# A two-layer hybrid transformer block on one core: where the recurrence's query decays and running totals are computed

## The chip, the cores and the metric

One core of a Trainium2 chip runs the whole program in one launch. The metric is the device time of one execution in microseconds (us), median of the runs shown. The engines are named as the profile names them: PE (TensorE, matrix products), PEld (its weight loads), DVE (VectorE), ACT (ScalarE), POOL (GpSimd) and SP (SyncE, which issues nearly all transfers).

## The reference

Two layers over 1024 latent tokens and 256 context tokens of width 1024. Each layer normalises, projects every token into eleven groups of columns (neighbourhood attention q, k, v; the recurrence's q, two forget gates, values and output gate; three inputs of a short convolution), mixes them in three ways, projects back, and runs a 16-expert layer. The change lies in the recurrence (HGRN2): six heads of 64 channels, forward and backward, a gated scan in chunks.

```python
def step(s, xs):
    qc, kc, gc, vc = xs
    a = jnp.cumsum(gc, axis=2)
    diff = a[:, :, :, None, :] - a[:, :, None, :, :]
    decay = jnp.exp(jnp.where(causal[:, :, None], diff, -jnp.inf))
    scores = jnp.sum(qc[:, :, :, None, :] * kc[:, :, None, :, :] * decay, axis=-1)
    o = jnp.einsum('bhts,bhsv->bhtv', scores, vc) + jnp.einsum('bhtk,bhkv->bhtv', qc * jnp.exp(a), s)
    ...
    s_new = jnp.exp(a_last[:, :, 0, :, None]) * s + jnp.einsum('bhsk,bhsv->bhkv', kc * jnp.exp(a_last - a), vc)
    return s_new, o
```

## The kernel before

A layer runs in stages: normalisation (`norm1`), the mixers' projections with the recurrence and the convolution (`mixers_in`), the projections for attention (`na_proj`), attention (`na_prep`, `na_pair`), the output projection, the experts. The program is recorded in this order, and then a scheduler that plays it through with its own table of costs decides in which order each engine's instructions stand; at run time each engine takes them strictly in that order. So the matmuls of the projections (`proj_ch`, L277, and `proj_tok`, L288, both writing `pj`) stand between the small products of the recurrence on PE.

The recurrence of a layer: three pairs of heads (`hg_pair`, p = 0, 1, 2), in each pair two heads one after the other, in each head two groups of 640 tokens (`hg_group`, g = 0, 1), whose instructions the scheduler interleaves. That makes 12 groups a layer and 24 in all. Channels of the forward direction lie in partitions 0 to 63 (`lo`), those of the backward direction in 64 to 127 (`hi`). A group goes through seven levels, h = 1, 2, 4, ..., 64, and at each level pairs of neighbouring blocks of h tokens are joined:

- up to h = 16, the half of the keys that is wanted is copied into `kz` (ACT L354, DVE L355), PE multiplies `kz` with the queries `Qt` (`small`, 20 products of 32x32, L341) and DVE merges the result into `Pc` (L357). At h = 32 and 64 PE multiplies `Kt` and `Qt` directly (L365) and ACT and DVE copy out (`Pf`, L370, L372).
- then half of the keys is multiplied by the neighbouring block's total decay (DVE, two instructions of 64x320, L375 and L376), half of the queries likewise (POOL, two of 64x320, L377 and L378), and the totals of neighbouring blocks are multiplied into the totals of the next level (`tot`, POOL L380, of 128x320 at the first level and half as wide at each further one).

The products of the next level read the new `Qt`, and the new `Qt` may only be written once the products of this level have read the old. After the levels the keys are transposed (L388), multiplied with the values (L393), and the states `S` are chained on DVE (`hg_states`, L411). When both heads of a pair are done, PE forms the outputs `ho` (L493, L496) and their mean squares `hms` (L505), DVE takes the reciprocal (L508), POOL multiplies (L509) and SP stores `mix`.

`wgroup` splits each weight into a high and a low part for the projections: `whi` on ACT (L264), `wlo` on DVE (L265). After the last pair of heads the convolution (`conv`, DVE L546 and L549, POOL L539 and L556) uses the recurrence's buffers. When these are released, attention's tables (`cw`, `sw`, L609 and L610) and its inputs (`qk`, L661) are loaded, normalised (`nsq`, `nss`, `nrsy`, `qd`) and transposed on PE (`nt`, L697). In attention's first part PE also forms the modulation vectors (`aps`, L157) from weights `wm` that SP loads (L153).

Of the kernel before, what the change touches and what calls it, by code (L numbers as in the profile page):

```python
# [15 lines left out]
ALU = mybir.AluOpType  # L16
# [26 lines left out]
class Kern:  # L43
# [283 lines left out]
    def hg_group(self, l, hd, g, F, Kt, Qt, S):  # L327


        nc, hp = self.nc, self.hp  # L330
# [3 lines left out]
        lo, hi = slice(0, 64), slice(64, 128)  # L334
# [14 lines left out]
        while h < P:  # L349
            n2 = G // (2 * h)  # L350
            v = lambda t: t.rearrange("p (n two h) -> p n two h", two=2, h=h)
# [21 lines left out]
            tv = tot.rearrange("p (n two) -> p n two", two=2)  # L373
            bc = lambda s, i: tv[s, :, i:i + 1].to_broadcast([64, n2, h])
            nc.vector.tensor_tensor(v(Kt)[lo, :, 0], v(Kt)[lo, :, 0], bc(lo, 1), ALU.mult)  # L375
            nc.vector.tensor_tensor(v(Kt)[hi, :, 1], v(Kt)[hi, :, 1], bc(hi, 0), ALU.mult)  # L376
            nc.gpsimd.tensor_tensor(v(Qt)[lo, :, 1], v(Qt)[lo, :, 1], bc(lo, 0), ALU.mult)  # L377
            nc.gpsimd.tensor_tensor(v(Qt)[hi, :, 0], v(Qt)[hi, :, 0], bc(hi, 1), ALU.mult)  # L378
            nt = hp.tile([P, n2], F32, name=f"tot{h}", bufs=1 if h < 64 else 4)
            nc.gpsimd.tensor_tensor(nt, tv[:, :, 0], tv[:, :, 1], ALU.mult)  # L380
            tot = nt
            h *= 2

# [1155 lines left out]
```

## Time and profile before

| | |
|---|---|
| median of 3 runs | 2754.39 us (2744.39 to 2755.64) |
| the profiled execution | 2748.93 us, span 2747.2 us |
| granted TensorE clock, mean | 0.959 of full speed |
| PE busy | 2520.3 us, 92% of the span |
| DVE busy | 1800.3 us, 66% |
| ACT busy | 1132.7 us, 41% |
| POOL busy | 1050.2 us, 38% |
| recurrence, layer 0 | about 165 to 572 us |
| recurrence, layer 1 | about 1613 to 2004 us |

PE's busy time counts an instruction from its start to a modelled end. A wait is put down to the instruction whose signal came last. The windows of the two layers run from the first product of the first head to the last `hms`.

### The profile page before, as it was taken

Reading aid. Unit: us, or ns where it says so; the run is one execution under the profiler, and the core shown is the slowest. Engines: PE = TensorE matmul, PEld = TensorE weight load, DVE = VectorE, ACT = ScalarE, POOL = GpSimd, SP = SyncE. Lnnn points to the kernel's source line nnn. Section 1 sums busy time; section 2 is a strip of 40 time slices with the busy share of each in tenths; the row PEclk is TensorE's granted clock in tenths of the full one; section 3 lists DMA queues with packets and bytes.
Section 4 is the critical chain, followed back from the end, with each engine's and each line's share of the span. In section 5 each row is a group of like instructions: output and inputs, shape, how many; then the busy total and the mean of one; then the engine's idle time right before and its main releaser. Section 6 shows DMA issues by size and latency. Waiting matters only on the chain.

```text
span 2747.2 us, 55415 instructions
## 1 busy us (share of the span) xinstructions
PE 2520.3 (92%) x21959; PEld 1923.8 (70%) x21959; DVE 1800.3 (66%) x3542; ACT 1132.7 (41%) x1878; POOL 1050.2 (38%) x1125
## 2 busy tenths in 40 slices
PE   7999999988999979999997999999879899589997
PEld 4988877885577855555554988778864677357664
DVE  4247776756777487777754347677767774687874
ACT  4224434324554534444433324344324454445452
POOL 1035454534544733323321035355554442222242
PEclk9999999998999979999998999999989899789999
DMA  7332324246444857888887332323176355779994
GB/s 277 104 105 71 103 72 124 64 140 209 150 141 148 302 190 261 285 271 296 262 279 231 90 109 72 114 76 103 50 208 222 100 164 185 283 269 369 378 376 129
DMA packets 347938, 507.14 MB, mean 185 GB/s; under 512 B 53380, under 2 KB 203072, under 8 KB 346592
## 3 DMA queue, kind: packets, MB, share of 16 engines
q1 hardware_dynamic: 336416, 465.85, 50.1%
q0 software_dynamic: 11264, 37.75, 5.9%
q8 instruction: 173, 2.83, 0.4%
q14 instruction: 85, 0.70, 0.1%
HBM read 410.10 MB, written 94.90 MB: 184 GB/s over the span
## 4 chain that ended last, share of the span: by engine, by line
PE 71%; DVE 15%; DMA 5%; issue 3%; ACT 2%; POOL 2%; SPq 1%; POOLq 0%; DVEq 0%; ACTq 0%
PE pj L277 15%; PE pg L1280 13%; PE pd L1335 8%; PE pj L288 8%; PE po L828 6%; PE nao L786 3%; PE npt L762 2%; PE pgc L1265 2%; DVE Kt L375 2%; PE aps L157 2%; PE hl L341 1%; PE sA L733 1%; DVE Kt L376 1%; DVE kz L355 1%; PE hl L365 1%
## 5 line engine op out<-in xcount | busy, mean ns | idle before, releaser
L1182 DVE TENSOR_TENSOR ewl<-est,ewh 128x2048 fp32r<-128x2048 f32 x126 | 298.3, 2371 | 112.6 <-ACT ewh L1178 108.1
L1178 ACT CAST ewh<-est 128x2048 fp32r<-128x2048 f32 x128 | 243.5, 1906 | 173.6 <-PE pg L1280 122.6
L277 PE MATMUL pj<-hl,whi 128*128 128x320 f32 (+2 forms) x912 | 314.2, 345 | 0.0
L277 PE MATMUL pj<-hh,whi 128*128 128x320 f32 (+2 forms) x912 | 312.5, 343 | 0.7 <-ACT pev L420 0.7
L277 PE MATMUL pj<-hh,wlo 128*128 128x320 f32 (+2 forms) x912 | 312.9, 343 | 0.0
L288 PE MATMUL pj<-whi,hh 128*128 128x256 f32 x960 | 279.8, 292 | 8.8 <-ACT nev L566 8.5
L288 PE MATMUL pj<-whi,hl 128*128 128x256 f32 x960 | 276.4, 291 | 0.9 <-DVE hl L239 0.9
L288 PE MATMUL pj<-wlo,hh 128*128 128x256 f32 x960 | 276.3, 289 | 0.0
L1335 PE MATMUL pd<-est,hidT 128*128 128x512 f32 x512 | 232.2, 596 | 2.1 <-ACT hidT L1302 2.1
L288 PEld LDWEIGHTS pj<-whi,hh 128*128 128x128 f32 x960 | 187.7, 195 | 12.0 <-ACT nev L566 9.3
L288 PEld LDWEIGHTS pj<-wlo,hh 128*128 128x128 f32 x960 | 187.5, 195 | 2.2 <-issue 1.5
L288 PEld LDWEIGHTS pj<-whi,hl 128*128 128x128 f32 x960 | 185.7, 195 | 3.8 <-DVE hl L239 1.5
L377 POOL TENSOR_TENSOR Qt<-Qt,tot 64x320 f32<-64x320 f32 x144 | 128.8, 894 | 150.9 <-PE hl L341 93.5
L277 PEld LDWEIGHTS pj<-hh,whi 128*128 128x128 f32 x912 | 174.8, 192 | 14.4 <-ACT pev L420 1.0
L277 PEld LDWEIGHTS pj<-hl,whi 128*128 128x128 f32 x912 | 174.9, 192 | 14.0 <-issue 1.2
L277 PEld LDWEIGHTS pj<-hh,wlo 128*128 128x128 f32 x912 | 175.0, 192 | 13.7 <-issue 1.4
L752 POOL TENSOR_SCALAR S<-S,sm 128x768 f32<-128x768 f32 (+2 forms) x108 | 112.7, 1045 | 186.3 <-DVE sm L751 153.2
L1335 PEld LDWEIGHTS pd<-est,hidT 128*128 128x128 f32 x512 | 95.2, 189 | 110.7 <-issue 103.3
L265 DVE TENSOR_TENSOR wlo<-wst,whi 128x1024 fp32r<-128x1024 f32 (+1 forms) x72 | 81.6, 1149 | 138.5 <-ACT whi L264 137.7
L1280 PE MATMUL pg<-ewh,xh 128*128 128x512 f32 x512 | 157.0, 425 | 2.9 <-ACT xh L1235 2.8
L1280 PE MATMUL pg<-ewl,xh 128*128 128x512 f32 x512 | 147.6, 404 | 0.0
L375 DVE TENSOR_TENSOR Kt<-Kt,tot 64x320 f32<-64x320 f32 x144 | 96.5, 670 | 76.7 <-POOL tot L380 39.6
(369 smaller groups left out, 5857.5 us busy)
## 6 DMA issues: line engine op xcount, KB each, us to landing
est<-in_w_exp_gate_dram SPq DMA_DIRECT2D x64, 1024.0 KB
est<-in_w_exp_up_dram SPq DMA_DIRECT2D x64, 1024.0 KB
est<-in_w_exp_down_dram SPq DMA_DIRECT2D x64, 1024.0 KB
wm<-in_w_mod_dram SPq DMA_DIRECT2D x80, 512.0 KB
wst<-in_w_in_dram SPq DMA_DIRECT2D x88, 256.0 KB
pna<-nev SPq DMA_DIRECT2D x180, 64.0 KB
wos<-in_w_out_dram SPq DMA_DIRECT2D x42, 256.0 KB
mst<-mix SPq DMA_DIRECT2D x32, 320.0 KB
```

What stands on the lines that cost most here:

```text
L265: nc.vector.tensor_tensor(b, c, a, ALU.subtract)
L277: nc.tensor.matmul(ps[:, :cn], sel(a(k)), b[:, k, c0:c0 + cn], start=n == 0, stop=n == 3 * KD - 1)
L288: nc.tensor.matmul(ps[:, :2 * P], b[:, k, t * P:(t + 1) * P], a(k).rearrange("p a n -> p (a n)"), start=n == 0, stop=n == 3 * KD - 1)
L375: nc.vector.tensor_tensor(v(Kt)[lo, :, 0], v(Kt)[lo, :, 0], bc(lo, 1), ALU.mult)
L377: nc.gpsimd.tensor_tensor(v(Qt)[lo, :, 1], v(Qt)[lo, :, 1], bc(lo, 0), ALU.mult)
L752: nc.gpsimd.tensor_scalar(S[:, :w], S[:, :w], sm[:, 1:2], 1.0, ALU.mult, ALU.mult)
L786: nc.tensor.matmul(po[64 * X:64 * X + 64, gi], V[:kn, tt, 64 * X:64 * X + 64], PT[X][:kn, i], start=i == 0, stop=i == len(ch) - 1, tile_po ...
L828: nc.tensor.matmul(ps, a, b, start=n == 0, stop=n == len(ops) - 1)
L1178: nc.scalar.copy(hi, src)
L1182: nc.vector.tensor_tensor(lo[:, :m], src[:, :m], hi[:, :m], ALU.subtract)
L1280: nc.tensor.matmul(acc[gu], a[:, 4 * hf + k], b[:, 512 * k:512 * k + 512], start=n == 0, stop=n == 3 * KD - 1)
L1335: self.downed = nc.tensor.matmul(po[nn], hT[:, 2 * hf + k], st[:, c:c + 512], start=hf == 0 and k == 0, stop=hf == 1 and k == 1)
```

## The change

The two multiplications of `Qt` by the decays and the multiplication of the totals, at every level of every group, are issued to VectorE instead of GpSimd. Operands, sizes and count stay: 14 multiplications of 64x320 and 7 of `tot` a group.

```diff
@@ -374,10 +374,10 @@
             bc = lambda s, i: tv[s, :, i:i + 1].to_broadcast([64, n2, h])
             nc.vector.tensor_tensor(v(Kt)[lo, :, 0], v(Kt)[lo, :, 0], bc(lo, 1), ALU.mult)
             nc.vector.tensor_tensor(v(Kt)[hi, :, 1], v(Kt)[hi, :, 1], bc(hi, 0), ALU.mult)
-            nc.gpsimd.tensor_tensor(v(Qt)[lo, :, 1], v(Qt)[lo, :, 1], bc(lo, 0), ALU.mult)
-            nc.gpsimd.tensor_tensor(v(Qt)[hi, :, 0], v(Qt)[hi, :, 0], bc(hi, 1), ALU.mult)
+            nc.vector.tensor_tensor(v(Qt)[lo, :, 1], v(Qt)[lo, :, 1], bc(lo, 0), ALU.mult)
+            nc.vector.tensor_tensor(v(Qt)[hi, :, 0], v(Qt)[hi, :, 0], bc(hi, 1), ALU.mult)
             nt = hp.tile([P, n2], F32, name=f"tot{h}", bufs=1 if h < 64 else 4)
-            nc.gpsimd.tensor_tensor(nt, tv[:, :, 0], tv[:, :, 1], ALU.mult)
+            nc.vector.tensor_tensor(nt, tv[:, :, 0], tv[:, :, 1], ALU.mult)
             tot = nt
             h *= 2
```

The scheduler gives another order for it, and not on DVE and POOL alone.

DVE in layer 1, first head of the third pair, one group at h = 4 and the other at h = 1 (`Pc` is the merge of a level's products, `hmm` its mask). Before:

```order
L357 COPY_PREDICATED Pc<-hmm_16124,hl 128x160
L375 TENSOR_TENSOR Kt<-Kt,tot_20464 64x160x2
L376 TENSOR_TENSOR Kt<-Kt,tot_20464 64x160x2
L357 COPY_PREDICATED Pc<-hmm_16116,hl 128x160
L355 COPY kz_16152<-Kt 64x80x4
L375 TENSOR_TENSOR Kt<-Kt,tot_20494 64x80x4
L376 TENSOR_TENSOR Kt<-Kt,tot_20494 64x80x4
```

The same place now:

```order
L357 COPY_PREDICATED Pc<-hmm_16124,hl 128x160
L377 TENSOR_TENSOR Qt<-Qt,tot_20235 64x80x4
L378 TENSOR_TENSOR Qt<-Qt,tot_20235 64x80x4
L355 COPY kz_16152<-Kt 64x80x4
L357 COPY_PREDICATED Pc<-hmm_16116,hl 128x160
L377 TENSOR_TENSOR Qt<-Qt,tot_20464 64x160x2
L378 TENSOR_TENSOR Qt<-Qt,tot_20464 64x160x2
L376 TENSOR_TENSOR Kt<-Kt,tot_20295 64x20x16
L380 TENSOR_TENSOR tot_20494<-tot_20464 128x160
L375 TENSOR_TENSOR Kt<-Kt,tot_20494 64x80x4
L376 TENSOR_TENSOR Kt<-Kt,tot_20494 64x80x4
```

Each merge is now followed by the two query decays of its group, and a total stands right ahead of the key decays that read it.

PE in layer 1, where the projections end and attention's transposes begin. Before, 240 matmuls of L288 stand between the last `hms` (L505) and the first transposes (`nt`). There the rows are

```order
L288 MATMUL pj<-whi,hl 128x256
L697 MATMUL nt<-idf,qd 128x128 x20
L735 MATMUL sB<-KH,QT 128x256
L735 MATMUL sB<-KL,QT 128x256
L157 MATMUL aps<-wm,sT 32x512 x6
L697 MATMUL nt<-idf,qd 128x128 x8
```

Now 46 matmuls of L288 are left after the last `hms`, and the rows are

```order
L288 MATMUL pj<-whi,hl 128x256
L157 MATMUL aps<-wm,sT 32x512 x8
L697 MATMUL nt<-idf,qd 128x128 x4
L157 MATMUL aps<-wm,sT 32x512 x8
L697 MATMUL nt<-idf,qd 128x128 x8
L157 MATMUL aps<-wm,sT 32x512 x2
```

So 194 matmuls of the projections have moved ahead of the recurrence's end, and 16 of the modulation ahead of most of the first transposes. At the same place of layer 0 it is 444 before and 310 now, and the modulation stays behind.

SP in layer 1, behind the last store of the recurrence's output. Before:

```order
L510 DMA mix_15766<-hos 128x512
L568 DMA pna_15767<-nev 128x128 x2
L596 DMA naw<-in_na_q_norm_dram 128x64
L597 DMA naw<-in_na_k_norm_dram 128x64
L609 DMA cw<-in_rope_dram 128x4x64
```

Now:

```order
L510 DMA mix_15766<-hos 128x512
L869 DMA wr<-in_w_router_dram 128x8x16
L637 DMA E<-rpbx 64x14x64 x4
L596 DMA naw<-in_na_q_norm_dram 128x64
L597 DMA naw<-in_na_k_norm_dram 128x64
L609 DMA cw<-in_rope_dram 128x4x64
```

The stores of the projections (`pna`) are done by then, and the loads of `wr` and `E` have come ahead of the tables.

## Rows read from the trace of the kernel before

**Rows 1.** The page: busy time by engine, and PE's row of the forty slices.
```profile
PE 2520.3 (92%) x21959; PEld 1923.8 (70%) x21959; DVE 1800.3 (66%) x3542; ACT 1132.7 (41%) x1878; POOL 1050.2 (38%) x1125
...
PE   7999999988999979999997999999879899589997
```

**Rows 2.** Windows: both recurrences, then two heads; span; busy us by engine; clock; transfers.
```profile
165.40:572.30 406.90, 380.08 (x5756) 339.27 (x5755) 294.51 (x518) 163.49 (x346) 208.74 (x269) 0.97 0.30 89
1613.00:2004.40 391.40, 367.21 (x5544) 321.07 (x5532) 291.75 (x529) 153.31 (x327) 205.31 (x270) 0.97 0.29 88
...
165.40:216.40 51.00, 46.13 (x832) 42.72 (x831) 37.01 (x66) 20.07 (x44) 29.56 (x36) 0.97 0.30 89
216.40:291.50 75.10, 71.81 (x1036) 66.18 (x1035) 49.62 (x100) 30.14 (x68) 34.59 (x52) 0.98 0.22 67
```

**Rows 3.** PE's longest wait in the recurrence of layer 0: us, times, longest.
```profile
PE hl L341 <- DVE kz L355: 19.6, 11, 3.6
```

**Rows 4.** One line's instructions (L377, L375, L376, L355, L411): min/median/max ns.
```profile
L377 POOL TENSOR_TENSOR Qt<-Qt,tot x144: 719/860/1620, 176.4 to 1977.0; 64x320 f32<-64x320 f32 x144
...
L375 DVE TENSOR_TENSOR Kt<-Kt,tot x144: 418/484/1834, 173.7 to 1977.0; 64x320 f32<-64x320 f32 x144
L376 DVE TENSOR_TENSOR Kt<-Kt,tot x144: 482/492/1309, 174.2 to 1978.6; 64x320 f32<-64x320 f32 x144
L355 DVE COPY kz<-Kt x120: 318/400/1170, 123.7 to 1962.0; 64x320 f32<-64x320 f32 x120
...
L411 DVE SCALAR_TENSOR_TENSOR S<-S,tot x216: 268/284/1636, 217.0 to 1989.3; 64x64 f32<-64x64 f32 x108
```

**Rows 5.** Timeline of DVE, then of POOL, head 0: start us, us.
```profile
176.67 1.06 DVE L375 TENSOR_TENSOR Kt<-Kt,F 64x320 f32<-64x320 f32 x1
177.76 1.07 DVE L376 TENSOR_TENSOR Kt<-Kt,tot 64x320 f32<-64x320 f32 x1
...
176.44 0.94 POOL L377 TENSOR_TENSOR Qt<-Qt,tot 64x320 f32<-64x320 f32 x1 [3.01 <-PE hl L341]
```

**Rows 6.** Groups of DVE in the recurrence of layer 1: busy us, mean ns.
```profile
L375 DVE TENSOR_TENSOR Kt<-Kt,tot 64x320 f32<-64x320 f32 x72 | 48.2, 670 | 41.6 <-POOL tot L380 19.3 <-PE hl L365 15.9 <-issue 5.4
L376 DVE TENSOR_TENSOR Kt<-Kt,tot 64x320 f32<-64x320 f32 x72 | 45.5, 632 | 2.1
L411 DVE SCALAR_TENSOR_TENSOR S<-S,tot 64x64 f32<-64x64 f32 x108 | 41.5, 384 | 14.4 <-ACT S L401 7.5 <-ACT S L396 3.7
L355 DVE COPY kz<-Kt 64x320 f32<-64x320 f32 x59 | 30.4, 517 | 1.5
...
L357 DVE COPY_PREDICATED Pc<-hmm,hl 128x160 f32<-128x160 uint8 x60 | 20.3, 338 | 6.7 <-PE hl L341 5.2
L508 DVE RECIPROCAL hrs<-hrs 128x512 f32<-128x512 f32 x5 | 16.7, 3349 | 11.8 <-ACT hrs L507 11.7
```

**Rows 7.** The chain of waits in both layers: start us, us, products and projection matmuls.
```profile
246.73 0.90 PE hl L341 x74
247.63 3.12 PE pj L277 x20
...
1985.57 6.04 PE pj L288 x50
```

**Rows 8.** Timeline at the end of layer 1's projections: the last hms, first transposes, first wm.
```profile
2003.94 1.02 PE L505 MATMUL hms<-hsq,hones 128*128 128x512 f32 x2
...
2040.88 1.09 PE L697 MATMUL nt<-idf,qd 128*128 128x128 f32 x4 [5.90 <-DMA pna<-nev]
...
2047.13 2.16 SPq L153 DMA_DIRECT2D wm<-in_w_mod_dram  x4
```

**Rows 9.** The same place in layer 0: POOL's first query block, and PE.
```profile
612.47 1.55 POOL L688 TENSOR_TENSOR qd<-qn,nrsy 128x512 f32<-128x512 f32 x1 [1.78 <-DVE nrsy L196]
...
634.68 0.60 PE L697 MATMUL nt<-idf,qd 128*128 128x128 f32 x4
```

**Rows 10.** The chain of waits at 2098 us: modulation matmuls (PE and its loads counted).
```profile
2101.88 0.98 PE aps L157 x4
```

## The prediction

> **What bounds the kernel now.** I read the page first: PE is busy 92% of the span, and in the stretches of the recurrence (slices 3 to 8 and 24 to 28) its row stands at 9 [rows 1]. Work that leaves POOL, busy 38%, is therefore worth only what PE waits for it. Next I read the two windows of the recurrence [rows 2]: in layer 0 PE is busy 380.1 of 406.9 us, in layer 1 367.2 of 391.4, both at a granted clock of 0.97. The idle time is 26.8 and 24.2 us, 51 us together, and no change inside the recurrence can give back more than this and a little clock. POOL is busy half of these windows (208.7 and 205.3 us), DVE three quarters (294.5 and 291.8). Then I read whom PE waits for: DVE's copy of `kz` heads the list with 19.6 us in 11 waits [rows 3], and nothing that POOL computes is on it. So the engine that gets the work is the one that PE waits for already.
>
> **DVE's bill.** Added, a group: 14 multiplications of 64x320 and 7 of totals. DVE's own multiplications of the same form, on `Kt`, have medians of 484 and 492 ns [rows 4]; I take 0.49 us, 6.9 us a group. The totals read 320, 160, ... 5 elements; at the slope of about 1 ns an element over some 0.16 us that the `Kt` rows give, they are 1.8 us. That is 8.7 us a group and 104 us a layer. The ends are 0.42 us (the least of L375) and 0.67 us (its mean in layer 1 now [rows 6]), 92 and 134 us a layer; I take the median because the mean holds what follows.
>
> Taken away: DVE is slow now because POOL runs beside it. While POOL works on `Qt`, the `Kt` multiplications take 1.06 and 1.07 us [rows 5]. With POOL quiet the groups of layer 1 fall to their medians or, for `kz`, its least: L375 72 x (670-484), L376 72 x (632-492), `kz` 59 x (517-318), `S` 108 x (384-284) ns [rows 4, 6], 13.4 + 10.1 + 11.7 + 10.8 = 46 us, and a few more for the first level; 50 us a layer. The ends are 0 (the slow ones are slow for another cause) and 50.
>
> So DVE's busy time grows by 104 - 50 = 54 us a layer, to some 348 of 407 and 346 of 391 us. About 250 more instructions a layer at 0.03 us between neighbours (176.67 + 1.06 to 177.76 [rows 5]) add 8. That still fits, at 88 to 91%, but not evenly.
>
> The Trainium skill (Perfetto Trace Analysis, Optimizing Scalar/DVE Operations) would send work the other way: with DVE saturated, ScalarE or even GpSimd should take some, though, as it adds, the two share a port and moving between them may not help. The rows bear out the second half: moving 104 us costs DVE 54.
>
> **Head by head.** In head 0 of layer 0 PE is busy 46.1 us of 51.0 and DVE 37.0 [rows 2]. Its bill becomes 37.0 + 17.4 (two groups) - 8.4 (a sixth of 50) + 3 (gaps of all its instructions) = 49 us, and the new order puts 206 instead of 213 projection matmuls into it, so that PE has 45 us to do. DVE is the longer by 4 us. In the second head, which also holds the gap until the next pair, DVE's bill is 49.6 + 12 = 62 against PE's 72 and more, so DVE is not the bound. The first head of each pair in layer 0 and of the last pair in layer 1 are of the first kind; in layer 1's other pairs the order has more matmuls to fill with. I price PE's idle time after the change at 4 us for each of those four heads and 2 to 2.5 for starts and steps in the other eight: 20 us in layer 0 instead of 27, **-7**, and 16 instead of 24 in layer 1, **-8**. Inside a level there is no reason for more: by the new order DVE does two merges, four query decays, a copy, a total and two key decays, 2 x 0.37 + 4 x 0.52 + 0.36 + 0.3 + 1.0 = 4.5 us with the gaps [rows 4, 6], while PE has two sets of products, 0.9 us, and 23 projection matmuls of L277 or 30 of L288, 3.6 us [rows 7]. What PE waits for stands in the first half of DVE's row. The weights' low parts (`wlo`), the `S` chain and the reciprocals are queued on the same DVE, and PE's projections wait for `wlo`; it is made a whole weight group ahead, and that cover I take to hold, at nothing. If it goes, a late `wlo` stalls PE as DVE's lag does in the rival below.
>
> **The end of the layer.** This is the term that the diff does not show. A projection matmul of L288 costs 6.04 / 50 = 0.121 us [rows 7]. In layer 1, 194 of them now stand ahead of the recurrence's end instead of behind it. Today, after the last `hms` (2003.9, done by 2004.4 [rows 2, 8]), 240 matmuls run to about 2035, while convolution, last store, tables, attention's inputs and their normalisation pass through DVE, POOL and SP; the first transposes start at 2040.9 after 5.9 us of idle [rows 8]. The path is 36.5 us, 30 of it under matmuls. With 46 matmuls only 5.6 us are under them. The recurrence ends 194 x 0.121 = 23.5 us later against PE's work, and so does attention start: **+23**. On SP the five issues of `wr` and `E` have come ahead of the tables, and the stores of `pna` that stood between are gone; the nearest row has four issues in 2.16 us [rows 8], so either is a few us, and I leave **+1**. In return 16 to 18 modulation matmuls, about 0.49 us each with their second pass [rows 10], can run in the hole once `wm` has landed; `wm` is issued today 42.7 us after the last `hms` [rows 8], now right behind `qk`. Part of these 8 us comes back later: **-5**.
>
> In layer 0, 134 matmuls (16.2 us) move likewise. There the first query block is ready at 614.0 and its transposes start at 634.7 [rows 9]: 20.7 us of slack, in which some waiting of the projections themselves is included. It covers the shift nearly: **+2**.
>
> **The sum.** -7 - 8 + 23 + 1 - 5 + 2 = +6 us. Against the profiled execution, 2748.9 us, this is 2755; that run lies 5.5 us below the median, 2754.4, and against the median it is **2760 us**, within the 0.5% (13.8 us) that a measurement of this kernel can tell from no change.
>
> **Rivals.**
> *The contention was the loss (faster).* The 51 us of idle time go down to 10 or so, since PE's waits are for `kz`, and `kz` takes 0.32 us alone and 0.52 on average [rows 4, 6]. Then -41 + 23 + 1 - 5 + 2 = -20, some 2734 us; with all 51 gone, 2724. For it: the waits for `kz` are where DVE is slow [rows 3, 6]. Against: DVE's bill is larger than PE's work in four heads.
> The Trainium skill states this side as a rule (GPSIMD Engine Reference, Engine selection): elementwise work belongs on VectorE, about twice as fast for two inputs. The prices agree, 860 to 484 ns. By it alone this rival would be the forecast.
>
> *DVE becomes the bound (slower).* If little of the 50 us comes back, or the query decays wait behind `wlo` and the reciprocals (3.3 us each [rows 6]) in DVE's order, DVE's bill is 294.5 + 104 + 8 = 407 us, all of layer 0's window. It decides once a pair of heads costs DVE more than PE, which is 46.1 + 71.8 = 118 us in the first pair [rows 2]. Head 0 would be bound by 12 instead of 4 us. With about 8 us more for each of the four heads and 2 us more for the others, +48, less my gain of 15 not had, and the tail in full: 2754 + 33 + 26 = 2813 us; half of it, 2785. For it: today the query decays run off DVE's queue, 2 x 0.86 us behind the products [rows 4]. Against: the overlap that slows DVE is plain instruction by instruction [rows 5].
>
> *The tail alone.* As forecast, but nothing comes back from the modulation and layer 0's slack does not hold (its slack is counted with a wait): 2760 + 5 + 8 = 2773.
>
> **Chances.** The balance as forecast 0.50, nearly all within 0.5%; the faster rival 0.17, of it 0.15 beyond 0.5%; DVE as the bound 0.20, nearly all beyond; the tail alone 0.13, on the slower side by a little. Faster 0.15, same 0.53, slower 0.32. The range for 8 in 10 reaches from the faster rival, 2734, to beyond the half of DVE's rival: 2734 to 2792.
>
> **What would show it.** Right: `Kt` decays near 0.49 us in the mean and `Qt` decays the same; DVE busy about 345 us in either recurrence, POOL under 20; PE's idle time there about 20 and 16 us; in layer 1 a hole of PE of some 25 us or more between the last L288 and the first transposes, with modulation matmuls in it, and next to none in layer 0. Wrong: `Kt` decays still at 0.6 us or more; PE's waits for `kz` or `Qt` above 30 us a layer; or attention of layer 1 starting as soon after the projections as now.

## The result, and the profile after

| | before | changed |
|---|---|---|
| median of the runs taken together | 2746.12 us (6 runs) | 2732.83 us (6 runs) |
| ratio to before | 1 | 0.9944, 95% interval 0.9931 to 0.9958 |
| the profiled execution | 2748.93 us, span 2747.2 us | 2732.13 us, span 2730.4 us |

By the ratio the change makes the kernel faster by 0.56%, some 15 us; the two medians lie 13.3 us apart. The interval, 0.42 to 0.69%, does not hold zero, and it lies on both sides of the 0.5% that the prediction took for the least difference. The forecast was no difference with a leaning to slower, 2760 us; the time lies 1.2 us below the lower end of the range. The three runs of before on which the forecast stood had a median of 2754.4 us; all later sets of before have medians of 2746 to 2750 us.

The page answers to [rows 1]. PE's row of slices is nearly the same; POOL has lost 381 us, and DVE has gained only 84:

```profile
PE 2504.4 (92%) x21959; PEld 1906.9 (70%) x21959; DVE 1884.3 (69%) x4046; ACT 1131.4 (41%) x1878; POOL 669.3 (25%) x621
...
PE   7999999998999979999996999999958899589997
```

The windows answer to [rows 2]: both recurrences, head 0, then in layer 1 the stretch from the last projection to the first transposes, and from there to the last `po` (L828). The columns are those of the rows before.

```profile
164.20:574.20 410.00, 391.62 (x5888) 351.05 (x5888) 333.21 (x764) 165.68 (x351) 19.27 (x22) 0.99 0.30 90
1599.10:2003.20 404.10, 387.18 (x5736) 339.18 (x5725) 331.50 (x773) 155.50 (x335) 17.60 (x23) 1.00 0.29 88
164.20:211.50 47.30, 44.80 (x824) 41.43 (x823) 41.22 (x97) 19.16 (x42) 0.00 (x0) 0.96 0.29 87
2009.00:2045.20 36.20, 4.91 (x19) 0.79 (x17) 13.95 (x27) 4.64 (x8) 18.13 (x24) 0.62 0.96 248
2045.20:2348.30 303.10, 284.40 (x1963) 203.80 (x1964) 210.65 (x526) 148.29 (x272) 124.82 (x114) 0.98 0.57 188
```

PE's idle time is span less busy: 18.4 us in layer 0 (26.8 before) and 16.9 in layer 1 (24.2), though 134 and 194 more projection matmuls lie in these windows. The granted clock went from 0.97 to 0.99 and 1.00. DVE is busy 333 and 332 us, POOL under 20. The fourth row is the hole that the order announced: 36.2 us, PE busy 4.9. The clock, 0.62 in the mean there between its two levels of 2.4 GHz (1) and 1.2 GHz, fell while PE stood idle; behind the hole it is 0.98.

In layer 1 two products stand some 17 us ahead of all the others (at 1595.9 us before, 1582.0 now). The windows of layer 1's recurrence begin behind them, at 1613.0 and 1599.1; the stages below that are counted from the first small product begin with them.

The groups of DVE in layer 1's recurrence answer to [rows 6]: busy us, mean ns.

```profile
L378 DVE TENSOR_TENSOR Qt<-Qt,tot 64x320 f32<-64x320 f32 x72 | 35.3, 490 | 1.4
L375 DVE TENSOR_TENSOR Kt<-Kt,tot 64x320 f32<-64x320 f32 x72 | 35.2, 489 | 7.3 <-PE hl L365 4.2 <-ACT kz L354 0.2
L376 DVE TENSOR_TENSOR Kt<-Kt,tot 64x320 f32<-64x320 f32 x72 | 35.1, 489 | 1.8
L377 DVE TENSOR_TENSOR Qt<-Qt,tot 64x320 f32<-64x320 f32 x72 | 34.5, 479 | 0.5
L411 DVE SCALAR_TENSOR_TENSOR S<-S,tot 64x64 f32<-64x64 f32 x108 | 31.5, 292 | 12.2 <-ACT S L401 9.3 <-ACT S L402 0.5
...
L357 DVE COPY_PREDICATED Pc<-hmm,hl 128x160 f32<-128x160 uint8 x60 | 20.2, 337 | 6.2 <-PE hl L341 5.0
L355 DVE COPY kz<-Kt 64x320 f32<-64x320 f32 x59 | 18.7, 323 | 0.9
```

`Kt` fell from 670 and 632 to 489 ns, `kz` from 517 to 323, `S` from 384 to 292; the merge `Pc`, which reads PSUM, stayed at 337. The query decays cost 479 and 490. With that PE's waits in layer 0 are short, where `kz` alone stood for 19.6 us [rows 3]; us, times, longest:

```profile
PE hl L341 <- DVE Qt L378: 7.5, 11, 1.3
...
PE hl L341 <- DVE kz L355: 1.5, 2, 0.9
```

In the hole PE stands idle until the modulation weights `wm` arrive; the first transposes come 7.5 us later, when `qd` is ready. Timeline of PE (the trace has two passes for each of these modulation matmuls, so these 16 are the eight of the order shown ahead of the prediction):

```profile
2037.74 4.65 PE L157 MATMUL aps<-wm,sT 128*32 128x512 f32 x16 [28.48 <-DMA wm<-in_w_mod_dram]
2045.23 1.11 PE L697 MATMUL nt<-idf,qd 128*128 128x128 f32 x4 [2.84 <-DVE qd L688]
```

### The profile page after: what moved, and what is told of

Same layout as the page of the kernel before. It is cut to its first block, busy times and chain, and to the rows that moved or that the text cites. A ratio compares the mean times of both kernels' runs of the same rounds, so it can differ in the third digit from the quotient of the medians.

```text
span 2730.4 us, 55190 instructions
## 1 busy us (share of the span) xinstructions
PE 2504.4 (92%) x21959; PEld 1906.9 (70%) x21959; DVE 1884.3 (69%) x4046; ACT 1131.4 (41%) x1878; POOL 669.3 (25%) x621
## 4 chain that ended last, share of the span: by engine, by line
PE 67%; DVE 18%; DMA 5%; issue 4%; ACT 3%; POOL 2%; SPq 1%; POOLq 0%; DVEq 0%; ACTq 0%
PE pg L1280 13%; PE pj L277 12%; PE pd L1335 8%; PE pj L288 8%; PE po L828 6%; PE nao L786 3%; PE pgc L1265 2%; PE npt L762 2%; PE sA L733 1%; DVE Kt L375 1%; PE aps L157 1%; DVE Kt L376 1%; DVE Qt L378 1%; PE hl L365 1%; PE xt L1231 1%
## 5 line engine op out<-in xcount | busy, mean ns | idle before, releaser
L288 PE MATMUL pj<-whi,hh 128*128 128x256 f32 x960 | 277.8, 290 | 4.5 <-ACT nev L566 4.1
L288 PE MATMUL pj<-whi,hl 128*128 128x256 f32 x960 | 276.8, 291 | 0.8 <-DVE hl L239 0.8
L288 PE MATMUL pj<-wlo,hh 128*128 128x256 f32 x960 | 275.5, 288 | 0.0
L1335 PE MATMUL pd<-est,hidT 128*128 128x512 f32 x512 | 232.2, 596 | 2.1 <-ACT hidT L1302 2.1
L288 PEld LDWEIGHTS pj<-whi,hh 128*128 128x128 f32 x960 | 186.0, 194 | 8.8 <-ACT nev L566 5.2
L288 PEld LDWEIGHTS pj<-wlo,hh 128*128 128x128 f32 x960 | 185.9, 194 | 2.2 <-issue 1.3
L288 PEld LDWEIGHTS pj<-whi,hl 128*128 128x128 f32 x960 | 184.6, 194 | 3.5 <-issue 1.3
L1335 PEld LDWEIGHTS pd<-est,hidT 128*128 128x128 f32 x512 | 95.2, 189 | 110.7 <-issue 103.3
L265 DVE TENSOR_TENSOR wlo<-wst,whi 128x1024 fp32r<-128x1024 f32 (+1 forms) x72 | 75.2, 1058 | 131.7 <-ACT whi L264 130.6
L1280 PE MATMUL pg<-ewh,xo 128*128 128x512 f32 x512 | 142.3, 398 | 2.1 <-DVE xo L1236 2.1
L750 ACT ACTIVATE S<-S,mn 128x768 f32<-128x768 f32 (+2 forms) x108 | 98.6, 913 | 85.2 <-DVE mn L745 79.6
```

Of the source, the lines that this page charges most:

```text
L265: nc.vector.tensor_tensor(b, c, a, ALU.subtract)
L288: nc.tensor.matmul(ps[:, :2 * P], b[:, k, t * P:(t + 1) * P], a(k).rearrange("p a n -> p (a n)"), start=n == 0, stop=n == 3 * KD - 1)
L750: nc.scalar.activation(S[:, :w], S[:, :w], AF.Exp, scale=-1.0, bias=mn[:, 1:2], accum_out=sm[:, 0:1])
L1280: nc.tensor.matmul(acc[gu], a[:, 4 * hf + k], b[:, 512 * k:512 * k + 512], start=n == 0, stop=n == 3 * KD - 1)
L1335: self.downed = nc.tensor.matmul(po[nn], hT[:, 2 * hf + k], st[:, c:c + 512], start=hf == 0 and k == 0, stop=hf == 1 and k == 1)
```

## The experiments

"Stretch" means, in layer 0, from the first small product to the last projection matmul. Times of a kernel are medians; stages and windows come from one traced execution each.

### Is it the engines or PE's order?

The change moves two things at once: the engine of 21 instructions a group, and by the scheduler the order of PE. So PE was held in one or the other order, each matmul queued behind its predecessor in a table of 16288 places, with no wait added. The order of the other engines was left to the scheduler.

```diff
+def in_order(nc, tc):
+    pe = [i for i in nc.cur_bb.bb.instructions if i.engine == mybir.EngineType.PE and type(i).__name__.startswith("InstMatmul")]
+    seq = [pe[a + k] for a, n in _ORD for k in range(n)]
+    for a, b in zip(seq[:-1], seq[1:]):
+        tc.add_manual_dep(b, a.name, mybir.DependencyInfo(mybir.DependencyClass.NoSync, mybir.DependencyReason.DATA),
...
         tile_kernel(tc, I, out)
+        in_order(nc, tc)
```

Engines of before, changed order:

> The kernel before (query decays and totals on GpSimd), but PE's instructions are held, all 16288 of them, in the order that the changed kernel has. Theory (what PE idles for is VectorE slowed by GpSimd; the order is a consequence): Kt decays stay above 0.6 us in the mean; in layer 0 the stretch from the first small product to the last projection stays at 465 to 475 us (before 469.2, changed 451.8); time 2745 to 2758 us. Rival (the new order is the gain: 134 more projection matmuls of L288 lie in the gaps of layer 0's recurrence): that stretch is 450 to 456 us, time 2731 to 2738 us.

Changed engines, order of before:

> The changed kernel, but PE's instructions are held in the order of the kernel before. Theory (contention): Kt decays at 0.49 us, layer 0's recurrence shortens by the 134 matmuls that leave it (16 us, to about 394 us), first small product to last projection 450 to 456 us, time 2730 to 2738 us. Rival (the order): recurrence about 407 us as before, stretch 465 to 472 us, time 2743 to 2755 us.

Measured, ratio to before with its interval, and stages from the four traces in us:

| engines | PE order | time, ratio | stretch, layer 0 | layer 1: first small product to last projection | from there to first transposes | first transposes to last `po` |
|---|---|---|---|---|---|---|
| GpSimd | before | 2747.8, 1 | 469.1 | 438.8 | 6.2 | 320.8 |
| GpSimd | changed | 2752.2, 1.0019 [1.0006, 1.0032] | 463.0 | 435.7 | 35.9 | 301.5 |
| VectorE | before | 2738.0, 0.9965 [0.9954, 0.9975] | 458.1 | 434.6 | 5.2 | 321.4 |
| VectorE | changed | 2732.8, 0.9944 [0.9931, 0.9958] | 451.7 | 427.0 | 36.3 | 303.1 |

Windows, the stretch and, for the two mixed kernels, the recurrence within it. GpSimd in the changed order:

```profile
165.50:628.50 463.00, 437.41 (x6199) 395.66 (x6198) 317.56 (x550) 172.17 (x367) 224.05 (x289) 0.97 0.31 93
165.50:586.90 421.40, 398.63 (x5890) 357.09 (x5890) 298.99 (x520) 164.80 (x351) 207.20 (x269) 0.97 0.30 88
```

VectorE in the order of before:

```profile
164.80:622.90 458.10, 432.57 (x6199) 391.58 (x6198) 351.38 (x795) 172.63 (x367) 39.57 (x46) 0.98 0.32 95
164.80:562.00 397.20, 377.59 (x5756) 336.84 (x5755) 329.24 (x763) 162.94 (x345) 20.26 (x22) 0.99 0.31 92
```

And the changed kernel:

```profile
164.20:616.00 451.80, 430.69 (x6199) 389.88 (x6198) 353.28 (x795) 173.21 (x367) 35.99 (x42) 0.99 0.32 95
```

The groups of the key decays in layer 0, GpSimd in the changed order and then VectorE in the order of before:

```profile
L375 DVE TENSOR_TENSOR Kt<-Kt,tot 64x320 f32<-64x320 f32 x72 | 49.7, 691 | 35.8 <-POOL tot L380 17.4 <-PE hl L365 11.1 <-issue 5.5
...
L375 DVE TENSOR_TENSOR Kt<-Kt,tot 64x320 f32<-64x320 f32 x72 | 35.1, 488 | 5.1 <-PE hl L365 1.6 <-ACT kz L354 0.6
```

In layer 0 the engines are worth 11 us of the stretch in either order (469.1 to 458.1, 463.0 to 451.7), and the order 6 us with either engines. The seven traced executions that have the changed engines and the changed order in layer 0 put the stretch at 448.0 to 453.6 us, so 11 us are clear of this spread; the order's 6 us are less so. Up to layer 0's last `po` the engines are worth 10.5 and 12.2 us, the order only 1.2 and 2.9: attention takes most of the order's part back.

The order alone makes the kernel no faster, it is 4.5 us slower. The engines alone make it 10 us faster; the traced execution of this kernel, 2731.4 us, lies 6.5 us under its median, so its stages are rather short. That the order adds something to the engines is not shown by the times: the intervals of 0.9965 and 0.9944 overlap. So the gain goes with the engines, and `Kt` is slow or quick with them in either order (691 and 488 ns). The theory's claim that the order is only a consequence does not stand for the stretch, which is 2 us under and 2 us over the expected bounds.

### Is it GpSimd's reading that slows VectorE?

Beside the changed kernel GpSimd did useless work at each level into a tile `dm` of its own, once with reads and once without:

```diff
+            nc.gpsimd.tensor_copy(self.dm[:, 0, 0:1], tot[:, 0:1])
+            for s in (lo, hi):
+                nc.gpsimd.tensor_tensor(self.dm[s], self.hones[s, 0:64].unsqueeze(1).to_broadcast([64, 5, 64]), self.hones[s, 0:64].unsqueeze(1).to_broadcast([64, 5, 64]), ALU.mult)
...
```

```diff
+            nc.gpsimd.tensor_copy(self.dm[:, 0, 0:1], tot[:, 0:1])
+            for s in (lo, hi, lo, hi):
+                nc.gpsimd.memset(self.dm[s], 0.5)
...
```

> The changed kernel, and beside it on GpSimd at each level two multiplications of 64x320 that read constants from SBUF and whose result nobody uses, kept in step by a copy of one column of the totals. PE's order in layer 0 is that of the changed kernel. Theory (contention): VectorE is slowed again: Kt decays at 0.6 us or more in the mean, VectorE busy 360 us or more in layer 0's recurrence (333 now), PE idle 25 us or more, time 2748 to 2775 us, since VectorE now carries the query decays as well. Rival (the order, or the place of the query decays, makes the gain, the slow instructions cost nothing): 2729 to 2737 us as without the added work.

> The changed kernel, and beside it on GpSimd at each level four fills of 64x320 that read nothing from SBUF, kept in step by the same copy of one column of the totals. PE's order is that of the changed kernel throughout. Theory (what slows VectorE is a GpSimd instruction that reads operands, not a busy GpSimd): Kt decays stay within 0.49 to 0.52 us, PE idle 17 to 20 us in layer 0's recurrence, time 2729 to 2738 us. Rival (any busy GpSimd slows VectorE): like the run with the reads, 2748 us or more.

Measured: with the reads 2807.5 us, 1.0223 [1.0206, 1.0240]; with the fills 2734.2 us, 0.9953 [0.9936, 0.9970], the changed kernel's time. Line numbers are shifted by one to four in these two kernels. Layer 0's recurrence with reads, as a window:

```profile
166.30:614.00 447.70, 404.19 (x5890) 361.34 (x5890) 388.65 (x765) 165.74 (x352) 173.69 (x252) 0.96 0.28 83
```

Its groups of DVE, busy us and mean ns:

```profile
L415 DVE SCALAR_TENSOR_TENSOR S<-S,tot 64x64 f32<-64x64 f32 x108 | 45.6, 423 | 6.3 <-ACT S L405 3.5 <-ACT S L406 0.3
L376 DVE TENSOR_TENSOR Kt<-Kt,tot 64x320 f32<-64x320 f32 x72 | 44.1, 613 | 7.1 <-PE hl L366 2.8 <-ACT kz L355 1.4
L377 DVE TENSOR_TENSOR Kt<-Kt,tot 64x320 f32<-64x320 f32 x72 | 42.5, 591 | 1.9
...
L356 DVE COPY kz<-Kt 64x320 f32<-64x320 f32 x59 | 21.8, 374 | 3.3 <-ACT Kt L472 2.6
L358 DVE COPY_PREDICATED Pc<-hmm,hl 128x160 f32<-128x160 uint8 x60 | 20.3, 338 | 1.6 <-PE hl L342 0.4
```

And the group of POOL that was added:

```profile
L382 POOL TENSOR_TENSOR dm<-hones 64x320 f32<-64x320 f32 x152 | 128.5, 846 | 10.5
```

With fills, the window:

```profile
166.70:579.80 413.10, 395.96 (x5890) 355.21 (x5890) 333.88 (x765) 165.17 (x351) 156.34 (x404) 0.98 0.30 90
```

Its groups of DVE:

```profile
L376 DVE TENSOR_TENSOR Kt<-Kt,tot 64x320 f32<-64x320 f32 x72 | 35.2, 489 | 11.2 <-PE hl L366 5.9 <-ACT kz L355 2.5
...
L415 DVE SCALAR_TENSOR_TENSOR S<-S,tot 64x64 f32<-64x64 f32 x108 | 31.4, 291 | 16.0 <-ACT S L405 12.6 <-ACT S L400 0.5 <-ACT S L406 0.5
...
L358 DVE COPY_PREDICATED Pc<-hmm,hl 128x160 f32<-128x160 uint8 x60 | 20.3, 338 | 3.5 <-PE hl L342 2.4
...
L356 DVE COPY kz<-Kt 64x320 f32<-64x320 f32 x59 | 19.5, 335 | 3.3 <-ACT Kt L472 2.6
```

And the added group of POOL:

```profile
L382 POOL MEMSET dm<- 64x320 f32 x304 | 111.3, 366 | 16.9
```

POOL is busy 174 and 156 us, so its being busy is not what counts. Beside the reads `Kt` takes 613 and 591 ns, `S` 423; beside the fills 489 and 291, as in the changed kernel. PE's idle time is 43.5 us against 17.1. The fills are also the shorter instructions, 366 against 846 ns; whether the length matters beside the reading was not tried apart. The loss with the reads is 32 us larger than the upper end of what was expected, 2775 us: VectorE, which carries the query decays as well, is busy 389 us of a recurrence that has grown from 410 to 448, so this run does not size the contention of the kernel before.

### Which of the moved instructions?

Only the query decays, then only the totals, against the changed kernel:

```diff
-            nc.vector.tensor_tensor(nt, tv[:, :, 0], tv[:, :, 1], ALU.mult)
+            nc.gpsimd.tensor_tensor(nt, tv[:, :, 0], tv[:, :, 1], ALU.mult)
```

```diff
-            nc.vector.tensor_tensor(v(Qt)[lo, :, 1], v(Qt)[lo, :, 1], bc(lo, 0), ALU.mult)
-            nc.vector.tensor_tensor(v(Qt)[hi, :, 0], v(Qt)[hi, :, 0], bc(hi, 1), ALU.mult)
+            nc.gpsimd.tensor_tensor(v(Qt)[lo, :, 1], v(Qt)[lo, :, 1], bc(lo, 0), ALU.mult)
+            nc.gpsimd.tensor_tensor(v(Qt)[hi, :, 0], v(Qt)[hi, :, 0], bc(hi, 1), ALU.mult)
```

> Only the two query decays of a level go to VectorE, the totals stay on GpSimd. Theory (VectorE and GpSimd slow each other, and PE idles for that): nearly the whole gain, since the query decays are what runs beside VectorE longest: Kt decays at 0.49 to 0.53 us in the mean, PE idle about 18 to 21 us in layer 0's recurrence (before 26.8, after 18.4), time 2731 to 2738 us. Rival (what helps is a queue: VectorE no longer waits for a total that GpSimd makes behind two query decays): the totals are still made on the other engine but now without the query decays ahead of them, so this cannot tell much here; the next run does.

> Only the totals go to VectorE, the query decays stay on GpSimd. PE's order is that of before for the first 12940 of 16597 instructions. Theory (contention): no gain, since the query decays still run beside VectorE: Kt decays stay above 0.6 us in the mean, PE idle 24 to 28 us in layer 0's recurrence, time 2743 to 2752 us. Rival (the totals' queue on GpSimd was the loss): Kt starts earlier, half or more of the gain, 2733 to 2739 us.

The totals alone: 2751.3 us, 1.0019 [1.0004, 1.0035], no gain, as the theory has it. Groups of DVE in layer 0, first one of the kernel before and then two of this run, with `Kt` still slow:

```profile
L375 DVE TENSOR_TENSOR Kt<-Kt,tot 64x320 f32<-64x320 f32 x72 | 48.3, 671 | 35.1 <-POOL tot L380 20.3 <-PE hl L365 7.3 <-issue 6.5
...
L376 DVE TENSOR_TENSOR Kt<-Kt,tot 64x320 f32<-64x320 f32 x72 | 52.5, 730 | 1.9
L375 DVE TENSOR_TENSOR Kt<-Kt,tot 64x320 f32<-64x320 f32 x72 | 51.2, 712 | 16.2 <-PE hl L365 13.2
```

VectorE no longer waits for GpSimd's totals, 20.3 us before, and nothing is gained: that queue was not the loss.

The query decays alone: 2753.0 us, 1.0020 [1.0008, 1.0032]. That is 15 us above the expected range, yet its stretch in layer 0 is 451.8 us, as short as the changed kernel's. Its recurrence in layer 0, and a piece of layer 0's experts:

```profile
164.60:568.70 404.10, 386.52 (x5847) 345.95 (x5847) 315.05 (x684) 164.74 (x350) 48.48 (x99) 0.99 0.30 89
1104.00:1386.00 282.00, 282.00 (x1465) 144.96 (x1464) 202.19 (x262) 118.31 (x121) 75.74 (x60) 1.00 0.84 273
```

Most of the loss lies in the experts. From layer 0's last `po` to layer 1's first small product it takes 622.7 us, where all other runs take 608.4 to 611.8. PE is busy throughout, 1465 matmuls in 282 us. The scheduler had chosen another order of PE's instructions there. So the same engines ran, with `in_order` and its table, under the changed kernel's order, and under a third order, which is the changed one to the end of layer 0 and that of before from there on; beside them the full change in that third order:

> Only the query decays on VectorE, the totals on GpSimd, with PE held in the changed kernel's order throughout. Theory (the query decays alone carry the gain; the run with the query decays alone lost 13 us in layer 0's experts to another order of PE there, which the scheduler chose): 13 us back in the experts (609 us from the last L828 of layer 0 to layer 1's first small product, against 623), time 2730 to 2738 us. Rival (totals on GpSimd cost the time somewhere else): 2743 us or more.

> Only the query decays on VectorE, and PE's order as in the run that joins the changed order of layer 0 with that of before. If both theories of the two runs beside this hold, it is equal to the first of them, 2724 to 2731 us; where the totals on VectorE still help (18 us of VectorE's time a layer against what GpSimd disturbs with them), it is 2 to 6 us slower than that.

> The changed kernel with PE held in the changed kernel's order until the end of layer 0 and in the order of before from there on. Theory (engines and order are two terms that add, layer by layer: the changed order helps layer 0 by 6 us and costs layer 1 some 5 us net, by its longer tail): layer 0 as in the changed kernel (first small product to last projection 452 us), layer 1 as in the run with all of before's order (first small product to last L828 761 us, changed 766), time 2724 to 2731 us, under both kernels. Rival (the layers depend on each other, or the difference of the tails is noise): 2732 us or more.

| engines | PE order | time | ratio to before |
|---|---|---|---|
| query decays on VectorE | changed | 2730.1 us | 0.9928 [0.9912, 0.9943] |
| query decays on VectorE | joined | 2723.9 us | 0.9896 [0.9879, 0.9912] |
| both on VectorE | joined | 2736.6 us | 0.9946 [0.9932, 0.9961] |

The same two windows of the query decays alone in the changed order:

```profile
166.80:572.80 406.00, 390.43 (x5890) 350.06 (x5890) 318.77 (x688) 165.22 (x351) 51.28 (x101) 1.00 0.31 92
1103.80:1386.00 282.20, 282.20 (x1515) 153.30 (x1508) 206.13 (x265) 120.14 (x123) 93.03 (x61) 1.00 0.84 279
```

1515 matmuls in the piece of the experts instead of 1465, and 611.8 us for the whole stage: 11 of the 13 us come back with PE's order there. Another 9 come back in layer 1 up to its last `po` (770.5 to 761.1 us); the scheduler's own order had no modulation matmul in the hole there. The totals on VectorE thus gain nothing. In the joined order they cost time, 2736.6 against 2723.9 us with intervals apart; DVE is busy 319 instead of 333 us in layer 0's recurrence where POOL keeps them. In the changed order the two intervals overlap.

The full change in the joined order missed its expectation, and the time is the rival's, 2732 us or more: layer 0 is right (451.4 us), but layer 1 gains only 2.5 us up to the last `po` and loses 3.0 behind it, so that the order of layer 1 is worth nothing to it. The query decays alone in the joined order have the lowest time of the study. At 2723.9 us it is the number that was expected, but not the reason, since the full change in this order, to which it should be equal, is 13 us slower. Its interval touches that in the changed order at 0.9912.

### The layers, and layer 1's tail

The change in one layer alone (the other run has `l == 1`; the three multiplications are then issued by `qe`):

```diff
+        qe = nc.vector if l == 0 else nc.gpsimd
...
```

> The change in layer 0 alone. PE's order is that of the changed kernel until layer 1. Theory (layer 0 gives the net gain; layer 1's gain in the recurrence is spent in its longer tail): 12 to 16 us under the kernel before, 2730 to 2734 us. Rival (both layers give half): 2737 to 2740 us.

> The change in layer 1 alone. PE's order is that of before until layer 1. Theory: recurrence 11 us shorter than its matmuls would ask, tail 29 us longer, some 20 us of it given back in attention: 0 to 4 us under the kernel before, 2742 to 2747 us. Rival (both layers give half): 2737 to 2740 us.

Layer 0 alone 2736.8 us, 0.9960 [0.9945, 0.9975]; layer 1 alone 2750.2 us, 1.0001 [0.9991, 1.0011]. The median for layer 0 alone lies 2.8 us above what was expected, right at the edge of the rival's range, and that for layer 1 alone 3.2 above; but the rival asked half of the gain of layer 1 too, which has none. The gain is layer 0's.

What the hole in layer 1 does was asked in four runs. First the last projections held behind the recurrence, then the loads of `E` put behind those of `qk` (`wr`, which the expectation names too, stayed where it was):

```diff
+            self.hms = nc.tensor.matmul(pm[:, :n], self.hones, sq[:, :n], start=True, stop=True)
...
-            self.tok(l, wp, a, b, ((0, P, self.pna, a), (P, 2 * P, self.pna, b)))
+            with self.tc.issue_after(self.hms.ins) if l == 1 and a == 256 else nullcontext():
+                self.tok(l, wp, a, b, ((0, P, self.pna, a), (P, 2 * P, self.pna, b)))
```

```diff
+                self.qkld = nc.sync.dma_start(qk[:, s], pv[:, t0:t0 + n, 384 * s + P * hp_:384 * s + P * hp_ + P])
...
-        EB = [self.na_bias(l, 2 * hp_ + X, ns) for X in range(2)]
+        with self.tc.issue_after(self.qkld.ins) if l == 1 and hp_ == 0 else nullcontext():
+            EB = [self.na_bias(l, 2 * hp_ + X, ns) for X in range(2)]
```

> The changed kernel, and in layer 1 the last group of attention's projections (240 matmuls of L288) is held behind the last hms, so that as many stand there as before; PE's order is that of the changed kernel until then. Theory A (the exposed tail is a loss of its own size, as predicted: 194 x 0.121 = 23 us, little of it given back): PE's hole shrinks from 36 us to under 12, the end comes 12 to 20 us earlier, 2713 to 2721 us. Theory B (the hole is paid back, by modulation matmuls run in it and a better clock after it): the hole closes, but attention takes 15 us more, time 2727 to 2734 us.

> The changed kernel, and in layer 1 the loads of E and wr, which SP issues in 6.5 us ahead of attention's tables, stand behind the loads of qk instead. Theory (the tail's path runs through SP's queue, and I priced this at 1 us where the trace shows 6.5): first transposes 5 to 7 us earlier after the last hms (42.0 us now), time 3 to 6 us less, 2727 to 2730 us. Rival (something else, GpSimd or the modulation weights, ends last): under 2 us earlier, time the same within 3 us.

Held projections: 2753.8 us, 1.0022 [1.0011, 1.0033], which neither theory had. The hole shrank to 12.4 us, but the recurrence became only 7 us shorter for 23 us of matmuls fewer, with 28 us of idle PE:

```profile
1598.00:1995.50 397.50, 369.54 (x5557) 320.09 (x5543) 328.67 (x771) 152.52 (x327) 13.98 (x20) 0.97 0.29 85
```

And attention, from the first transposes to the last `po`, took 334.8 us, 31.7 more, in an order in which PE waits, among others, so:

```profile
PE nt L698 <- DMA nav<-pna: 12.1, 1, 12.1
PE nt L698 <- POOL qd L689: 8.2, 1, 8.2
```

Another order with as many projections behind the recurrence takes 321.4 us there (VectorE in the order of before, table above), so the further 13 us come with this one order of attention; which of its places cost them was not tried.

Loads of `E` put later: 2747.8 us, 0.9996 [0.9987, 1.0006], 15 us slower than the change. The hole stayed at 36.2 us, as the rival had it, though its time (within 3 us) missed. The issues have a part in the path all the same. VectorE had its last `nss` 2.4 us sooner after the last `hms`, but from there to `qd` it took 8.3 instead of 6.0 us: GpSimd's multiplication of `E` now fell beside this chain of short instructions. One of 40 elements, where the one ahead of it with the same shape (L189) took 0.18 us, ended together with it:

```profile
2034.44 1.94 DVE L191 TENSOR_SCALAR nrsy<-nrss 128x40 int32<-128x40 int32 x1
...
2034.26 2.08 POOL L639 TENSOR_TENSOR E<-E,cm 128x896 f32<-128x896 f32 x1 [4.84 <-DMA E<-rpbx]
```

And no modulation matmul ran in the hole any more, and attention took 315.2 us instead of 303.1. The next run does that alone:

```diff
+        nt0 = K.ntl
...
-                        K.adaln(l, [1, 2], ap)
+                        with tc.issue_after(nt0.ins) if l == 1 else nullcontext():
+                            K.adaln(l, [1, 2], ap)
```

> The changed kernel, and in layer 1 the modulation matmuls stand on PE behind attention's first transposes, so that none runs in the hole. Theory (part of the tail's 29 us is given back because 18 modulation matmuls run in the hole and no longer between attention's own): hole 36 us as now, from the first transposes to the last L828 10 to 14 us longer (303.1 us now), time 2740 to 2748 us. Rival (attention became faster for another reason): that stretch within 4 us of 303, time 2731 to 2737 us.

Measured: 2747.5 us, 0.9997 [0.9987, 1.0007]. Windows of the hole and of attention:

```profile
2014.10:2050.10 36.00, 0.27 (x3) 0.09 (x2) 14.01 (x27) 4.64 (x8) 18.26 (x24) 0.57 0.89 221
2050.10:2365.30 315.20, 290.36 (x1979) 208.82 (x1980) 208.24 (x527) 148.45 (x272) 120.63 (x114) 0.95 0.56 185
```

The hole is as long, and attention again 315.2 us: 12 us come back in attention when modulation matmuls stand early. In the changed kernel eight of them run in the hole (the 16 passes of 4.65 us above) and eight more right behind the first transposes, and PE then waits 0.19 us for the second block of transposes. Here it waits 5.72 us, with nothing to fill:

```profile
2056.91 1.97 PE L697 MATMUL nt<-idf,qd 128*128 128x128 f32 x8 [5.72 <-POOL qd L688]
```

The run moves both eights, so what each gives back is not told apart. Of the 12.1 us, 6.1 are idle time of PE (24.8 against 18.7) and 6.0 busy time, at a clock of 0.95 against 0.98. The time lost, 15 us, is what the theory expected. More of them, sooner, by issuing `wm` from ACT:

```diff
-                    self.modlds.append(nc.sync.dma_start(t, I[
+                    qe = nc.scalar if l == 1 and r else nc.sync
+                    self.modlds.append(qe.dma_start(t, I[
```

> The changed kernel, and in layer 1 the modulation weights wm are issued by ACT, where they don't stand behind tables and qk in SP's queue; PE's order then has 16 modulation matmuls ahead of all first transposes and 10 more behind the first four. Theory (PE's hole waits for wm, 28.5 us, and what runs in it is given back later): the first aps starts 15 to 20 us after the last L288 instead of 28.7, time 2718 to 2728 us. Rival (the transfers, not their place in the queue, end last, or the loads slow down qk and the tables): 2730 us or more.

Measured: 2753.7 us, 1.0022 [1.0011, 1.0034]. Windows again:

```profile
2010.10:2060.30 50.20, 13.25 (x36) 1.62 (x34) 14.11 (x27) 4.43 (x8) 18.50 (x24) 0.59 0.89 243
2060.30:2367.70 307.40, 280.93 (x1946) 204.70 (x1947) 207.48 (x526) 148.59 (x272) 120.34 (x113) 0.98 0.53 176
```

The first `aps` starts 18.2 us after the last projection, as expected, and PE does 13 us of work in the hole, but the hole has grown to 50 us: the issues of `qk` begin 32.0 us after the last `hms` instead of 24.7, behind `E` and the tables. Then VectorE's `nss` waits 7.1 us for ACT's `nsq`, and ACT is late because it spends 25.7 us on issuing eight loads of `wm`; `nsq` starts when these are out. The rival was right.

## Why the prediction was wrong

Two terms of the sum failed, layer 0's gain and what attention gives back; each of the others came within 5 us. Term by term, measured between the same events of the two profiled executions, in us:

| term | forecast | measured |
|---|---|---|
| layer 0, first small product to last `po` (idle time and slack) | -7 + 2 | -13.4 |
| layer 1, recurrence against its matmuls | -8 | -10.8 |
| layer 1, tail laid open, with SP's issues | +23 + 1 | +29.0 |
| layer 1, given back in attention | -5 | -17.7 |
| everything else | 0 | -3.9 |
| sum | +6 | -16.8 |

**What bounds the kernel.** Right: PE, and what it waits for in the recurrence is DVE's slow `kz` and what stands ahead of it.

**DVE's bill.** The prices were right, that of the totals too, though the `Kt` rows have one size and cannot give the slope that it was worked out from (a total measured 493 ns at 320 elements, 160 at 5). The moved instructions sum to 102.6 us of durations in layer 1 (forecast 104), and the others got shorter by 51 (forecast 50), 48 of it `Kt`, `kz` and `S`. But busy time counts overlapping neighbours once: DVE's grew by 39.7 us, not 54, and the 8 us added for gaps between more instructions had the wrong sign. DVE had some 15 us more room in each recurrence than the prediction gave it. In head 0 it is busy 41.2 us, where the prediction had 49 with the gaps.

**The idle time.** 18.4 and 16.9 us, forecast 20 and 16. This step was right, and yet **the step that priced layer 0's gain by it alone failed**. Of the 17.4 us that the stretch gained, 8.4 are idle time. 4.7 are matmuls that ran faster: 380.1 + 134 x 0.121 = 396.3 us of work took 391.6, at a clock of 0.99. 4.3 lie behind the last `hms`, where PE's idle time fell from 6.8 to 2.7 us. The prediction called the clock "a little" and gave it no term. Attention then took 4.0 us of the 17.4 back, for which +2 stood.

**Layer 1's tail.** +23 was right: 194 x 0.121. The path from the last `hms` to the first transposes grew from 36.5 to 42.0 us, for which +1 stood. Of these 5.5 us, 4.3 lie ahead of the end of VectorE's `nss`, and the run with the loads of `E` put later takes 2.4 of them away; it gains nothing, since `E` then stands beside the normalisation.

**What is given back: the term that failed most.** -5 was forecast, "part of these 8 us"; 17.7 came back, more than the matmuls themselves take. Keeping them out of the hole and from behind the first transposes costs attention 12.1 us, so two thirds of it are theirs: in the changed kernel PE is idle in attention 18.7 us instead of 26.1 before and runs at 0.98 instead of 0.95. What the prediction left out is that they fill a wait of attention itself, and the clock. Together with layer 0 this is 21 of the 23 us by which the sum was off. The other third has no run of its own.

**The base.** 2760 and the range were counted from the median of three runs, 2754.4 us. From that of six, 2746.1, the same sum gives 2752, and a range shifted alike would have begun 8 us lower and held the measured time. That it lies outside is thus the base's doing; that the sum had the wrong sign is not.

**The rivals.** The first, that the contention was the loss, came true in sign and nearly in size (2734 us forecast, 2732.8 measured), but the number is luck: the two recurrences' idle time went to 35 us, not 10, attention gave back more than was counted, and the base was high. DVE did not become the bound. The run with the added reads comes nearest to it: of PE's 43.5 us of idle time some 33 are waits for DVE, though PE with 404 us is still busier than DVE with 389. The rule that the Trainium skill states for that side (GPSIMD Engine Reference, Engine selection), elementwise work on VectorE, holds in these runs for the query decays and not for the totals.

**What would show it.** `Kt` and `Qt` at 0.49 us, POOL under 20 us, the idle times, the hole in layer 1 and none in layer 0: all there. DVE at 345 us: not there, 333.

The cause is settled so far: with PE's order held, moving the instructions gives 11 us in layer 0; reads of GpSimd beside VectorE make it slow again, fills do not; the totals have no part in the gain. What is not told apart is how much of the 11 us comes from `Kt` and `kz` being quick again and how much from a query decay taking 0.49 instead of 0.86 us. PE's waits speak for the first: before, it never waited for GpSimd's `Qt` in layer 0, and 0.5 us in layer 1. For layer 1 the engines give 4 to 9 us up to the last projection. The scheduler's order is worth 1 to 3 us up to layer 0's last `po`; in layer 1 it costs a hole and gives most of it back. Over the whole kernel it costs 4.5 us with the engines of before, and with VectorE its gain is not clear of the noise.

The 3.9 us elsewhere lie mostly behind layer 1's last `po`: from there to the last `pd` (L1335) it is 369.5 us instead of 372.9, and every run with the changed order in layer 1 has 368.8 to 369.5 there, every run with that of before 371.8 to 372.9 (the held projections, an order of its own, 370.1). Why was not asked.

## What to carry to other kernels

Before moving an operation off a second engine, look for groups on the first whose mean lies well above their median: here nearly all of that surplus, 48 us a layer, came back with the move, and busy time grew by less than the sum of the durations. Move only what disturbs: here the long instructions that read SBUF beside the engine that PE waits for, not the short ones. Where a scheduler reorders the program on each edit, hold the order of the bounding engine fixed when comparing; a reordering far from the edit was worth 11 us here, nearly as much as the edit. And where an edit moves work away from a later stage, ask what that stage gets back: its waits and its clock, not only the work's own time.

## What the runs showed of the hardware

GpSimd working 156 us of a recurrence on fills left VectorE's two-input instructions as they were (`Kt` 489 ns, `S` 291) and `kz` nearly (335 against 324). Working 174 us, most of it with two SBUF operands, it lengthened `Kt` to 613, `S` to 423 and the single-input copy `kz` to 374 ns, but not the merge with its PSUM operand (337 to 339 in all these runs). The Trainium skill (SBUF — State Buffer, Who interferes with whom) says that a VectorE instruction with two SBUF inputs contends with a GpSimd instruction that reads SBUF and not with one that only writes; the runs agree. `kz`, with one input, is not what this sentence speaks of.

A short VectorE instruction can last as long as the GpSimd instruction beside it: in the run with `E` put later, two of 40 elements took 1.94 and 2.00 us and ended within 0.1 us of GpSimd's multiplications of 2.08 and 2.06 us.

PE's granted clock went roughly with its idle time in layer 0's recurrence: 0.96 with 43.5 us idle, 0.97 with 26.8, 0.99 with 18.4, 1.00 with 15.6 (the query decays alone in the changed order); not strictly, for it was 0.98 with 17.1 (the fills) and 0.97 with 22.8 (GpSimd in the changed order). From 0.97 to 0.99, the same work took PE 4.7 us less, on top of 8.4 us less idle time.
